# Moving the pool of small tiles ahead of the weight pools in a two-block network on one core

## The chip, the cores and the metric

The kernel runs on one core of a Trainium2 chip. The metric is device time in microseconds (us) of one execution of the whole kernel. Engines are written as in the profile: PE is TensorE (matmuls), PEld its loads of the stationary operand, DVE is VectorE, ACT is ScalarE, POOL is GpSimd, and SPq, ACTq and POOLq are the queues that issue DMAs.

## What is computed

The input is 512 tokens of width 1024, in float32. Two blocks follow each other. The first block is a dilated attention layer (three groups of eight heads, joined by their log-denominators, with a gate) and a differential attention layer (two softmaxes of which one is subtracted from the other), each between two RMS norms and with a residual. The second block is a feed-forward layer, a mixer of three gated branches (sparse attention with an index, a state-space layer, attention to 256 memory tokens), and a second feed-forward layer, with norms and residuals. Cut to what matters here, nearly all the arithmetic is projections of this form:

```python
def swiglu_ffn(h, w_in, w_out):
    gate, up = jnp.split(h @ w_in, 2, axis=-1)
    return (jax.nn.silu(gate) * up) @ w_out
...
x = x + 0.5 * swiglu_ffn(rms_norm(x, ffn1_norm[l]), ffn1_w_in[l], ffn1_w_out[l])
h = rms_norm(x, mix_norm[l])
q_a, k_a, v_a, q_i, k_i, w_i, u_s, q_m, gates = jnp.split(h @ w_in[l], offsets, axis=-1)
```

## The kernel before

**Projections.** Every product of an activation and a weight is made from three matmuls (`mm3`, lines 151 to 155): both operands are split into a high part h and a low part l in the type float32r, and h·h, h·l and l·h are added up in PSUM. Line 153 multiplies the high parts, line 154 and line 155 one high and one low part. A matmul has a stationary operand, which is loaded first (an LDWEIGHTS of 128 columns, shown as PEld), and a moving operand, which streams through. In the rows of the profile the moving operand is named first: `pp<-uh,wh` streams the activation uh past the weight wh, and `pp<-wh,uh` streams the weight past the activation.

There are two forms. `feat` (line 384) gives a feature-major result: the weight is stationary, 128 of its columns at a time, and 512 tokens of the activation move. `tok` (line 335) gives a token-major result: 128 tokens of the activation are stationary and up to 512 columns of the weight move. With `perm=True` (values of the dilated groups 1 and 2) the stationary tokens are taken four apart.

**Weights.** All weights come through one pipeline, in the order of a plan that is written out as the steps are set up. `_load` (line 291) issues, on the SP queue, the DMA of a piece of [128, 1024] into one of two buffers `raw`; `_split` (line 305) turns it into a pair `wh`, `wl` out of rings of four, with a cast on ACT (line 175) and a subtraction on DVE (line 176). A piece is split up to two pieces ahead of its use, and the load of a further piece is issued right after a split.

**Activations.** They lie transposed in rings `u` and `y` of [128, 4, 512] tiles (`uh`, `ul`, `yh`, `yl`). The 256 memory tokens have tiles of their own, `mT0h`, `mT0l`, `mT1h` and `mT1l`, of [128, 4, 256], out of the pool `aux` (line 1355); they are the stationary operand of one projection, `w_mem_kv`, in the form `tok`.

**Memory.** Pools are laid out end to end in each partition, in the order in which they are opened, and a pool that is opened takes its place behind those that are open. Lines 72 to 76 open the pools that stay open to the end:

```python
self.cpool = pool("consts", 1)
self.rings = {"u": pool("u", 2), "y": pool("y", 2)}
self.wraw = pool("wraw", RAW)
self.wsplit = pool("wsplit", RING)
self.small = pool("small", 2)
```

All other pools are opened later, behind `small`. `small` holds tiles of one to four numbers per partition (sums of squares, reciprocal roots), in 22 slots of 32 bytes, 704 bytes in all. Consts take 3,072 bytes, the four activation tags 16,384 each, `raw` 8,192, `wh` and `wl` 16,384 each. The places per partition that follow, in bytes:

| tile | first byte before | beyond a multiple of 128 |
|---|---|---|
| uh, ul, yh, yl | 19,584 / 35,968 / 52,352 / 68,736 | 0 |
| raw | 85,120 | 0 |
| wh, wl | 93,312 / 109,696 | 0 |
| small | 126,080 to 126,784 | 0 |
| mT0h, mT0l, mT1h, mT1l | 176,160 / 180,256 / 184,352 / 188,448 | 32 |

A piece of a matmul's operand is a whole number of times 512 bytes into its tile in nearly all cases: 128 stationary columns are 512 bytes. The exceptions are the projection of 452 columns (line 1462, `[(w, 512, 452)]`), whose second row of weights starts 1,808 bytes into the tile, and the stationary operand of the permuted form, whose columns are 16 bytes apart.

**Order of the work.** The host program emits the instructions in one order, with the estimated work of TensorE as its clock; side chains (attention, softmax, norms) are put between the matmuls of the projections by delays on that clock. Nothing in that order depends on where a tile lies.

## Time and profile before

| | |
|---|---|
| median of 3 runs | 2165.97 us (2165.5 to 2167.97) |
| profiled execution, first to last instruction | 2168.1 us |
| granted TensorE clock, mean | 0.994 |
| PE busy | 2108.8 us (97%), 10,217 matmul records |
| PEld busy | 1712.7 us (79%) |
| DVE busy | 1232.5 us (57%) |
| ACT busy | 938.7 us (43%) |
| POOL busy | 232.9 us (11%) |
| DMA | 204.11 MB, 94 GB/s on average |

The profiled execution's own time is known by its span alone, 2168.1 us, which is 2.1 us over the median of the runs. A matmul's duration in the profile (some 390 ns for 512 columns) is longer than the distance from one start to the next, since matmuls overlap; what the kernel pays for one matmul is the distance between starts, which the rows in order of time show.

### The profile page before, as it was taken

Reading aid. Unit: us, or ns where it says so; the run is one execution under the profiler, and the core shown is the slowest. Engines: PE = TensorE matmul, PEld = TensorE weight load, DVE = VectorE, ACT = ScalarE, POOL = GpSimd, SP = SyncE. Lnnn points to the kernel's source line nnn. Section 1 sums busy time; section 2 is a strip of 40 time slices with the busy share of each in tenths; the row PEclk is TensorE's granted clock in tenths of the full one; section 3 lists DMA queues with packets and bytes.
Section 4 is the critical chain, followed back from the end, with each engine's and each line's share of the span. In section 5 each row is a group of like instructions: output and inputs, shape, how many; then the busy total and the mean of one; then the engine's idle time right before and its main releaser. Section 6 shows DMA issues by size and latency. Waiting matters only on the chain.

```text
span 2168.1 us, 27642 instructions
## 1 busy us (share of the span) xinstructions
PE 2108.8 (97%) x10217; PEld 1712.7 (79%) x10217; DVE 1232.5 (57%) x2673; ACT 938.7 (43%) x1885; POOL 232.9 (11%) x322
## 2 busy tenths in 40 slices
PE   7999999999999999999999999988899999999998
PEld 6888988889888776788888888755567888888887
DVE  5645457454667677876443337889964345333334
ACT  4746455464545655555222224443344333223223
POOL 0000000000000000110960000125422110000000
PEclk9999999999999999999999999999999999999999
DMA  5322222212243212233343334222243323333332
GB/s 169 95 69 68 69 69 63 84 59 70 80 127 127 88 59 68 98 121 107 124 148 94 98 96 150 78 61 72 65 147 106 90 86 98 98 97 98 97 98 78
DMA packets 152055, 204.11 MB, mean 94 GB/s; under 512 B 9848, under 2 KB 111240, under 8 KB 151920
## 3 DMA queue, kind: packets, MB, share of 16 engines
q1 hardware_dynamic: 138368, 170.70, 25.8%
q10 hardware_dynamic: 8352, 15.14, 2.4%
q0 software_dynamic: 5200, 16.50, 2.2%
q8 instruction: 80, 1.31, 0.3%
q14 instruction: 55, 0.45, 0.1%
HBM read 191.80 MB, written 10.51 MB: 93 GB/s over the span
## 4 chain that ended last, share of the span: by engine, by line
PE 50%; DVE 8%; ACT 2%; issue 1%; DMA 1%; POOL 1%; ACTq 0%; DVEq 0%; POOLq 0%; SPq 0%
PE pp L153 15%; PE pp L154 15%; PE pp L155 15%; PE pa L159 3%; PE pa L164 2%; DVE wl L176 1%; DMA raw<-in_w_in 1%; DVE s5wr L1147 1%; DVE s5wi L1148 1%; DVE score L1262 1%; DVE m L1261 0%; DVE s5t L1150 0%; ACT p L438 0%; POOL s5wr L1142 0%; ACT wh L175 0%
## 5 line engine op out<-in xcount | busy, mean ns | idle before, releaser
L176 DVE TENSOR_TENSOR wl<-raw,wh 128x1024 fp32r<-128x1024 f32 (+1 forms) x320 | 407.1, 1273 | 495.5 <-ACT wh L175 494.2
L175 ACT CAST wh<-raw 128x1024 fp32r<-128x1024 f32 (+1 forms) x320 | 333.4, 1042 | 642.4 <-PE pp L154 291.3
L153 PE MATMUL pp<-uh,wh 128*128 128x512 f32 (+1 forms) x1232 | 485.1, 394 | 0.3 <-DVE sg L445 0.2
L154 PE MATMUL pp<-ul,wh 128*128 128x512 f32 (+1 forms) x1232 | 477.8, 388 | 1.0 <-DVE ul L282 1.0
L155 PE MATMUL pp<-uh,wl 128*128 128x512 f32 (+1 forms) x1232 | 477.8, 388 | 0.0
L153 PEld LDWEIGHTS pp<-uh,wh 128*128 128x128 f32 x1232 | 232.3, 189 | 52.0 <-issue 7.2
L155 PEld LDWEIGHTS pp<-uh,wl 128*128 128x128 f32 x1232 | 232.5, 189 | 45.9 <-issue 0.6
L154 PEld LDWEIGHTS pp<-ul,wh 128*128 128x128 f32 x1232 | 232.7, 189 | 43.7 <-DVE ul L282 1.2
L153 PE MATMUL pp<-wh,uh 128*128 128x512 f32 (+2 forms) x592 | 238.1, 404 | 0.0
L154 PE MATMUL pp<-wl,uh 128*128 128x512 f32 (+2 forms) x592 | 229.5, 388 | 0.2 <-DVE wl L176 0.2
L155 PE MATMUL pp<-wh,ul 128*128 128x512 f32 (+2 forms) x592 | 228.8, 387 | 0.0
L153 PE MATMUL pp<-yh,wh 128*128 128x512 f32 (+1 forms) x464 | 176.3, 380 | 0.8 <-DVE M L1497 0.8
L155 PE MATMUL pp<-yh,wl 128*128 128x512 f32 (+1 forms) x464 | 174.7, 377 | 0.0
L154 PE MATMUL pp<-yl,wh 128*128 128x512 f32 (+1 forms) x464 | 174.5, 376 | 0.0
L425 ACT COPY rq<-pp 32x512 f32<-32x512 f32 x256 | 147.8, 577 | 58.0 <-PE pp L155 52.8
L153 PEld LDWEIGHTS pp<-wh,uh 128*128 128x128 f32 x592 | 128.0, 216 | 20.3 <-issue 4.6
L154 PEld LDWEIGHTS pp<-wl,uh 128*128 128x128 f32 x592 | 128.5, 217 | 16.7 <-DVE wl L176 1.2
L155 PEld LDWEIGHTS pp<-wh,ul 128*128 128x128 f32 x592 | 127.6, 216 | 16.6 <-issue 0.3
L153 PE MATMUL pp<-wh,yh 128*128 128x512 f32 x304 | 119.1, 392 | 0.0
L154 PE MATMUL pp<-wl,yh 128*128 128x512 f32 x304 | 118.8, 391 | 0.0
L155 PE MATMUL pp<-wh,yl 128*128 128x512 f32 x304 | 118.7, 390 | 0.0
L438 ACT ACTIVATE sm<-sm,nm 128x128 f32<-128x128 f32 (+1 forms) x192 | 79.8, 417 | 54.4 <-DVE nm L437 54.1
(404 smaller groups left out, 2783.9 us busy)
## 6 DMA issues: line engine op xcount, KB each, us to landing
raw<-in_ffn_w_in SPq DMA_DIRECT2D x176, 256.0 KB, 3.1
raw<-in_dil_w_in SPq DMA_DIRECT2D x80, 512.0 KB, 3.6
raw<-in_ffn_w_out SPq DMA_DIRECT2D x44, 512.0 KB, 3.7
raw<-in_diff_w_in SPq DMA_DIRECT2D x32, 512.0 KB, 3.7
raw<-in_w_in SPq DMA_DIRECT2D x32, 512.0 KB, 3.7
raw<-in_dil_w_out SPq DMA_DIRECT2D x8, 512.0 KB, 3.7
raw<-in_diff_w_out SPq DMA_DIRECT2D x8, 512.0 KB, 3.7
s5tab<-s5cs POOLq DMA_DIRECT2D x8, 512.0 KB, 3.4
```

The lines of the kernel that those rows point to most:

```text
L153: mm(ps, a[0], b[0], start=first, stop=False)
L154: mm(ps, a[0], b[1], start=False, stop=False)
L155: mm(ps, a[1], b[0], start=False, stop=last)
L159: self.nc.tensor.matmul(ps, a, b, start=start, stop=stop)
L164: self.nc.tensor.transpose(ps, x, self.ident[:n, :n])
L175: self.nc.scalar.copy(h, src)
L176: return self.nc.vector.tensor_tensor(l, src, h.bitcast(F32), op=OP.subtract)
L425: nc.scalar.copy(sw[b:b + 32, :], ps[c][b ^ 32:(b ^ 32) + 32, :])
L438: nc.scalar.activation(sm, sm, AF.Exp, bias=nm, scale=-1.0, accum_out=den)
L1147: V.tensor_tensor_scan(wr, mag, wr, 0.0, op0=OP.mult, op1=OP.add)
L1148: V.tensor_tensor_scan(wi, mag, wi, 0.0, op0=OP.mult, op1=OP.add)
L1262: V.match_replace(sc[:, :n], m8, sc[:, :n], -BIG)
```

## The change

Two lines change places in what is computed: the pool `small` is opened before `wraw` and `wsplit`. The diff also takes comments and docstrings out (their lines stay as empty lines, so that line numbers hold).

```diff
         self.cpool = pool("consts", 1)
         self.rings = {"u": pool("u", 2), "y": pool("y", 2)}
+        self.small = pool("small", 2)
         self.wraw = pool("wraw", RAW)
         self.wsplit = pool("wsplit", RING)
-        self.small = pool("small", 2)
         self.pp = pool("pp", 4, space=PSUM)
```

So `raw`, `wh` and `wl` lie 704 bytes further on (85,824, 94,016 and 110,400), the tiles of `small` 40,960 bytes further back (at 85,120), and everything else, the rings of activations in front and all pools behind, where it was. 704 is five times 128 and 64 more.

## Rows read from the trace of the kernel before

**Rows 1.** The page: span, and busy time of each engine.
```profile
span 2168.1 us, 27642 instructions
...
PE 2108.8 (97%) x10217; PEld 1712.7 (79%) x10217; DVE 1232.5 (57%) x2673; ACT 938.7 (43%) x1885; POOL 232.9 (11%) x322
```

**Rows 2.** Busy time by stretch: length, PE, PEld, DVE, ACT, POOL, clock, DMA, GB/s.
```profile
960.00:1320.00 360.00, 359.68 (x1684) 300.19 (x1684) 161.97 (x242) 116.42 (x161) 100.46 (x171) 1.00 0.36 115
1345.00:1680.00 335.00, 305.83 (x1412) 216.97 (x1410) 270.44 (x634) 135.74 (x318) 101.56 (x99) 0.98 0.31 90
```

**Rows 3.** PE in order of time, first feed-forward: start, duration, line; 86 matmuls, first and last.
```profile
1130.69 0.39 PE L154 MATMUL pp<-ul,wh 128*128 128x512 f32 x1
...
1149.96 0.39 PE L155 MATMUL pp<-uh,wl 128*128 128x512 f32 x1
```

**Rows 4.** The same, second feed-forward, matmuls of 256 columns: 110, first and last.
```profile
1808.32 0.28 PE L155 MATMUL pp<-yh,wl 128*128 128x256 f32 x1
...
1821.40 0.28 PE L153 MATMUL pp<-yh,wh 128*128 128x256 f32 x1
```

**Rows 5.** The same, weight moving, activation stationary: 13 matmuls, first and last.
```profile
1182.14 0.39 PE L153 MATMUL pp<-wh,yh 128*128 128x512 f32 x1
...
1184.87 0.39 PE L153 MATMUL pp<-wh,yh 128*128 128x512 f32 x1
```

**Rows 6.** The same, weight moving, memory tile stationary: 13 matmuls, first and last.
```profile
1325.73 0.39 PE L153 MATMUL pp<-wh,mT0h 128*128 128x512 f32 x1
...
1328.53 0.39 PE L153 MATMUL pp<-wh,mT0h 128*128 128x512 f32 x1
```

**Rows 7.** The same, permuted form, stationary columns 16 bytes apart: 15 matmuls, first and last.
```profile
214.32 0.40 PE L155 MATMUL pp<-wh,ul 128*128 128x512 f32 x1
...
217.61 0.40 PE L154 MATMUL pp<-wl,uh 128*128 128x512 f32 x1
```

**Rows 8.** The same, 452 columns of weight moving: 18 matmuls, first and last.
```profile
1342.32 0.37 PE L153 MATMUL pp<-wh,uh 128*128 128x452 f32 x1
...
1345.79 0.37 PE L155 MATMUL pp<-wh,ul 128*128 128x452 f32 x1
```

**Rows 9.** The page, costliest groups: busy and mean ns, then idle time before.
```profile
L153 PE MATMUL pp<-uh,wh 128*128 128x512 f32 (+1 forms) x1232 | 485.1, 394 | 0.3 <-DVE sg L445 0.2
L153 PE MATMUL pp<-wh,uh 128*128 128x512 f32 (+2 forms) x592 | 238.1, 404 | 0.0
L153 PE MATMUL pp<-yh,wh 128*128 128x512 f32 (+1 forms) x464 | 176.3, 380 | 0.8 <-DVE M L1497 0.8
L153 PE MATMUL pp<-wh,yh 128*128 128x512 f32 x304 | 119.1, 392 | 0.0
```

**Rows 10.** Groups of the stretch 1345 to 1680, line 153, weight stationary.
```profile
L153 PE MATMUL pp<-uh,wh 128*128 128x512 f32 x147 | 61.7, 420 | 0.0
L153 PE MATMUL pp<-yh,wh 128*128 128x512 f32 x48 | 21.1, 443 | 0.8 <-DVE M L1497 0.8
```

**Rows 11.** Lines 175 and 176: durations ns min/median/max, first and last start, forms.
```profile
L175 ACT CAST wh<-raw x320: 602/1050/1077, 9.0 to 2139.0; 128x1024 fp32r<-128x1024 f32 x156, 128x904 fp32r<-128x904 f32 x2, 128x512 fp32r<-128x512 f32 x2
L175 ACT CAST yh<-sg x24: 387/617/621, 970.3 to 1292.0; 128x512 fp32r<-128x512 f32 x20, 128x256 fp32r<-128x256 f32 x4
L176 DVE TENSOR_TENSOR wl<-raw,wh x320: 679/1226/3009, 10.1 to 2140.1; 128x1024 fp32r<-128x1024 f32 x156, 128x904 fp32r<-128x904 f32 x2, 128x512 fp32r<-128x512 f32 x2
L176 DVE TENSOR_TENSOR yl<-sg,yh x24: 405/684/1774, 971.1 to 1293.6; 128x512 fp32r<-128x512 f32 x20, 128x256 fp32r<-128x256 f32 x4
```

**Rows 12.** The page, DMA issues: KB each, median us to landing.
```profile
raw<-in_diff_w_in SPq DMA_DIRECT2D x32, 512.0 KB, 3.7
s5cs<-s5tab ACTq DMA_DIRECT2D x8, 512.0 KB, 3.4
```

**Rows 13.** Waits, the SP queue's and PE's: us in total, times, longest.
```profile
SPq L300 <- DVE wl L176: 1546.0, 269, 25.3
...
PE pp L154 <- DVE wl L176: 0.2, 1, 0.2
```

## The prediction

> **What bounds the kernel now.** I read the page's busy times first. TensorE is busy 2108.8 of 2168.1 us and no other engine over 57% [rows 1], so a change counts by what it does to TensorE's spacing, or by a wait that it puts in front of TensorE. [...]

> Then the rows in order of time, for the price of one matmul from start to start. In the first feed-forward, 85 distances take 1149.96 - 1130.69 = 19.27 us, or 226.7 ns [rows 3]. With 256 columns, 109 distances take 13.08 us, or 120.0 ns [rows 4]. The 256 columns of difference cost 106.7 ns, which is one column per tick of 2.4 GHz; so 512 columns are 213.3 ns, and 13.3 ns stay as a pause that each matmul pays whatever its length. The pause is the same with the weight moving: twelve distances take 2.73 us [rows 5].

> Two stretches have another pause, and they are what this prediction turns on. Where the memory tiles are stationary, twelve distances take 2.80 us, 233.3 ns each [rows 6], with the same moving weights. The only thing I find that sets these matmuls apart is the place of the stationary operand, 32 bytes beyond a multiple of 128, where all activations and weights lie on one. In the permuted form, with the stationary columns 16 bytes apart, fourteen distances take 3.29 us, 235.0 ns each [rows 7]. So how the stationary operand lies in memory reaches the spacing: by 6.7 ns in one case, 8.3 ns in the other.

> **The change part by part.** No instruction is added, removed or moved, on an engine or a queue: the order is that of an emission which does not look at places. What changes is three addresses: raw, wh and wl start 64 bytes beyond a multiple of 128 instead of on one.

> Stationary weights. These are all matmuls of the form feat: per line of mm3 1,232 with uh and 464 with yh moving [rows 9], and three lines, so 3 x 1,696 = 5,088. No row of before has a float32r weight at 64 bytes beyond. The bounds are 0 (64 counts as on the grid) and 6.7 ns each (64 counts as the 32 of the memory tiles does). Nothing excludes a gain, but no row has a pause under 13.3 ns; a gain is taken up as a rival. I take the upper end, since the only contiguous stationary operand off 128 in the trace pays it, and all that are on 128 don't. In 1345 to 1680 us there are 3 x (147 + 48) = 585 of them [rows 10], in stretches with slack; I take 0 for these, with 585 x 6.7 ns = 3.9 us kept for the range. The other 4,503 stand back to back or nearly so: 4,503 x 6.67 ns = **30.0 us**. Nothing hides this, as TensorE is the bound there [rows 2].

> [...]

> Moving weights. The form tok has 592 with uh and 304 with yh per line [rows 9], 2,688 in all. The nearest row is the projection of 452 columns, in which half the moving weights start 1,808 bytes into a tile, 16 beyond a multiple of 128: 17 distances take 3.47 us, 204.1 ns; 452 columns are 188.3 ns, so the pause is 15.8 ns, 2.5 more than with all on 128 [rows 8]. If the half that is off bore it all, 5 ns each, 2,688 of them would cost 13.4 us; the lower bound is 0. I take 0: a length of 452 is itself odd, and a moving operand is one long stream in which the start matters little. The 13.4 us go to the range.

> Splits. The cast on ACT and the subtraction on DVE read and write tiles that all move together. A cast of 512 columns out of sg, which lies off 128 wherever it is placed, takes 617 ns, and the shortest out of raw, on 128, 602; the subtractions take 684 and 679 [rows 11]. So 15 ns and 5 ns per half piece are the upper bounds, 2 x 15 x 320 = 9.6 us of ACT and 3.2 us of DVE in all, and 0 the lower. I take 0: ACT and DVE work two pieces ahead, and TensorE waited 0.2 us once for a wl [rows 13]. Without that cover the 9.6 us would be paid.

> Loads. A 512 KB load into raw lands in 3.7 us, one of the same size into s5cs, which lies off 128, in 3.4 [rows 12]. So I take 0, with 0.3 us per load either way as the bound. The SP queue spends 1546 us waiting until DVE has freed a raw [rows 13], so loads have time to spare; that is the cover, and the split's lead of two pieces behind it.

> Small tiles. They move by 40,960 bytes, which is 320 x 128: nothing changes in how they lie, cost 0.

> Sum: 2168.1 + 30.0 = 2198.1 us on the profiled execution's span; that execution stands 2.1 us over the median of the runs shown, so 2166 + 30 = **2196 us** as a median.

> **The rivals.** *No change: 64 bytes are enough of a grid.* If what counts is a multiple of 64 (or less), the memory tiles pay because 32 is no multiple of 64, and weights at 64 beyond pay nothing. For it: both 32 and 64 are unknown steps, and the trace has one value only. It is also the outcome if another trait of the memory tiles (how far they lie from the weights, what else runs in that stage) makes their 6.7 ns, or if the shift does not reach the matmuls as the code says. Time 2166, 2162 to 2170. [...] *Both operands pay.* What counts is how the stationary and the moving operand lie to each other, so that tok pays as well: 4,503 + 2,688 = 7,191 times 6.7 ns, 48 us, 2214; or tok by the bound of [rows 8], 13.4 us, 2209. Against it: the 452 columns, whose weights lie 16 bytes off their activations and pay at most 5 ns. *Faster.* The pause of 13.3 ns is itself a clash of two streams that start alike, and an offset of 64 bytes takes half of it away: 6.7 ns less in 4,503 matmuls, 30 us, 2136. It decides as soon as a distance under 226.7 ns appears in the first feed-forward. Against it: neither offset in the trace, 32 for the stationary nor 16 for the moving operand, brought the pause down.

> **How the numbers follow.** Stationary weights pay: 0.48. Both pay: 0.06. No change: 0.38. Faster: 0.08. The first two are slower, 0.54. A measurement of this kernel can tell about 0.2% (4 us) from no change, so the shares stand as faster 0.08, same 0.38, slower 0.54. The range runs from the lower edge of "no change", 2162, to the forecast with the 3.9 us of the slack stretches and half of the moving operand's 13.4 us on top, some 2206; outside lie the 0.08 of faster and the 0.06 of both. The forecast's own range is 2185 to 2206, its lower end being two thirds of the price, where disturbed matmuls next to attention work pay nothing.

> **What would show it.** In the profile after, the same count of 27,642 instructions, and in the first feed-forward a distance of 233.3 ns where the weight is stationary, beside 226.7 where it moves. The memory tiles' stretch should stay at 233.3 if the stationary operand's place alone counts, and may move if it is the offset between both operands. ACT's casts stay at 1050 ns, DVE's subtractions at 1226, loads at 3.7 us. I am wrong if the weight-stationary distance stays at 226.7 (no change), falls (faster), or if the time goes up with these distances unchanged, which would mean a wait for loads or splits that I have put at nothing.

## The result and the profile after

The changed kernel takes 2187.28 us (2186.61 to 2189.62, 4 runs) against 2165.73 us before (4 runs): a ratio of 1.0097 with a 95% interval of 1.0083 to 1.0111, so 21.5 us slower, where 30 were forecast. The instructions of every engine stand in the same order as before.

The page after, span and busy time of each engine:

```profile
span 2185.4 us, 27642 instructions
...
PE 2126.9 (97%) x10217; PEld 1708.9 (78%) x10217; DVE 1227.7 (56%) x2673; ACT 938.4 (43%) x1885; POOL 233.6 (11%) x322
```

And the same two stretches as in [rows 2], with the same columns (length, PE, PEld, DVE, ACT, POOL, clock, DMA, GB/s):

```profile
960.00:1320.00 360.00, 358.54 (x1660) 295.85 (x1659) 155.48 (x231) 116.00 (x162) 100.47 (x169) 1.00 0.35 112
1345.00:1680.00 335.00, 303.84 (x1407) 215.88 (x1406) 270.78 (x639) 136.42 (x316) 98.77 (x97) 0.98 0.31 92
```

TensorE is busy 18.1 us longer than in [rows 1], no other engine by more than 0.7 us. The clock is as granted before, 1.00 and 0.98. But the same 360 us hold 1,660 matmuls instead of 1,684 [rows 2], with TensorE as good as always busy: on average a matmul takes longer.

Which ones, the rows in order of time show, as in [rows 3] (start, duration, line, operands with the moving one first). First, the first feed-forward with the weight stationary and uh moving, 84 matmuls:

```profile
1130.80 0.39 PE L153 MATMUL pp<-uh,wh 128*128 128x512 f32 x1
...
1149.80 0.39 PE L155 MATMUL pp<-uh,wl 128*128 128x512 f32 x1
```

Then the weight moving, the counterpart of [rows 5], 70 matmuls:

```profile
1189.85 0.39 PE L153 MATMUL pp<-wh,yh 128*128 128x512 f32 x1
...
1205.95 0.40 PE L153 MATMUL pp<-wh,yh 128*128 128x512 f32 x1
```

And in the second feed-forward the weight stationary again, with yh moving, 85 matmuls:

```profile
1982.22 0.40 PE L155 MATMUL pp<-yh,wl 128*128 128x512 f32 x1
...
2001.82 0.40 PE L155 MATMUL pp<-yh,wl 128*128 128x512 f32 x1
```

The distance from start to start is 19.00 / 83 = 228.9 ns in the first, 16.10 / 69 = 233.3 ns in the second and 19.60 / 84 = 233.3 ns in the third. Before, the first had 226.7 [rows 3]. The second begins with the row at 1182.14 of [rows 5], and its 70th matmul is the first row below: 15.65 / 69 = 226.8. The other two rows are the third before, the same 85 matmuls: 19.04 / 84 = 226.7.

```profile
1197.79 0.39 PE L153 MATMUL pp<-wh,yh 128*128 128x512 f32 x1
...
1969.20 0.39 PE L155 MATMUL pp<-yh,wl 128*128 128x512 f32 x1
...
1988.24 0.39 PE L155 MATMUL pp<-yh,wl 128*128 128x512 f32 x1
```

So the form in which the weight moves pays the full 6.6 to 6.7 ns, though the prediction gave it nothing, and the form in which it is stationary pays 2.2 ns in one place and 6.7 in another.

The memory tiles, stationary as in [rows 6], keep their distance: 13 matmuls after, 2.80 / 12 = 233.3 ns.

```profile
1336.15 0.39 PE L153 MATMUL pp<-wh,mT0h 128*128 128x512 f32 x1
...
1338.95 0.39 PE L153 MATMUL pp<-wh,mT0h 128*128 128x512 f32 x1
```

What does not move are the splits and the loads. The cast has a median of 1048 ns and the subtraction of 1225, against 1050 and 1226 [rows 11]. Lines 175 and 176 after:

```profile
L175 ACT CAST wh<-raw x320: 601/1048/1077, 8.8 to 2155.7; 128x1024 fp32r<-128x1024 f32 x156, 128x904 fp32r<-128x904 f32 x2, 128x512 fp32r<-128x512 f32 x2
...
L176 DVE TENSOR_TENSOR wl<-raw,wh x320: 676/1225/2353, 9.8 to 2156.8; 128x1024 fp32r<-128x1024 f32 x156, 128x904 fp32r<-128x904 f32 x2, 128x512 fp32r<-128x512 f32 x2
```

The loads land in 3.6 us, against 3.7 [rows 12]. From the page's DMA issues after:

```profile
raw<-in_diff_w_in SPq DMA_DIRECT2D x32, 512.0 KB, 3.6
```

**The account.** I took all distances under 260 ns between neighbouring matmuls of mm3 with 512 moving columns, from both traces, and multiplied the difference of the means by the number before. Weight moving: 227.4 to 233.3 ns, 2,016 times (33 of them past the memory tiles), 12.0 us. Permuted form: 235.4 to 237.9, 330 times, 0.8 us. Weight stationary, uh moving: 227.8 to 229.3, 3,162 times, 4.9 us. Weight stationary, yh moving: 227.0 to 230.6, 1,136 times, 4.0 us. Matmuls of fewer columns come to 0.2 us in all. That makes 21.9 us by means. The order of the matmuls is the same in both traces, so each distance can also be paired with its own counterpart. Paired so, these distances grew by 22.6 us, and the 3,018 that hold other work or a wait shrank by 5.1: together 17.5 us from TensorE's first start to its last, beside 17.3 us between the two spans. The rest up to 21.5 us lies in the choice of executions. A run's time is some 1.8 us more than its span wherever both are known (2187.24 and 2185.4 us for the one profiled after). By that the one profiled before, known by its span alone, took about 2169.9 us, an estimate, which is 4.2 us over its median and not the 2.1 that comes of setting a span beside a time; the one profiled after stands at its own median.

### The profile page after: what moved, and what is told of

It is laid out like the page before. It is cut to its first block, busy times and chain, and to the rows that moved or that the text cites. A ratio compares the mean times of both kernels' runs of the same rounds, so it can differ in the third digit from the quotient of the medians.

```text
span 2185.4 us, 27642 instructions
## 1 busy us (share of the span) xinstructions
PE 2126.9 (97%) x10217; PEld 1708.9 (78%) x10217; DVE 1227.7 (56%) x2673; ACT 938.4 (43%) x1885; POOL 233.6 (11%) x322
## 4 chain that ended last, share of the span: by engine, by line
PE 51%; DVE 8%; ACT 1%; DMA 1%; issue 1%; POOL 1%; ACTq 0%; DVEq 0%; SPq 0%; POOLq 0%
PE pp L153 15%; PE pp L154 15%; PE pp L155 15%; PE pa L159 3%; PE pa L164 2%; DVE wl L176 1%; DVE s5wr L1147 1%; DVE s5wi L1148 1%; DMA raw<-in_w_in 0%; DVE m L1261 0%; DVE score L1262 0%; DVE s5t L1150 0%; ACT p L438 0%; POOL s5wr L1142 0%; ACT wh L175 0%
## 5 line engine op out<-in xcount | busy, mean ns | idle before, releaser
L176 DVE TENSOR_TENSOR wl<-raw,wh 128x1024 fp32r<-128x1024 f32 (+1 forms) x320 | 400.9, 1253 | 508.4 <-ACT wh L175 507.4
L155 PEld LDWEIGHTS pp<-uh,wl 128*128 128x128 f32 x1232 | 232.8, 189 | 46.8 <-issue 0.6
L155 PE MATMUL pp<-wh,ul 128*128 128x512 f32 (+2 forms) x592 | 230.6, 390 | 0.0
L153 PEld LDWEIGHTS pp<-yh,wh 128*128 128x128 f32 x464 | 87.2, 188 | 21.4 <-issue 3.9
```

What stands on the lines that cost most here:

```text
L153: mm(ps, a[0], b[0], start=first, stop=False)
L155: mm(ps, a[1], b[0], start=False, stop=last)
L176: return self.nc.vector.tensor_tensor(l, src, h.bitcast(F32), op=OP.subtract)
```

## The experiments

Three theories stood at the start. **A:** what counts is how the two operands of a matmul lie to each other. **B:** each operand counts for itself, by its distance from a multiple of 128; this was the prediction's, with the moving operand added to it. **C:** the matmuls alone don't show it; something that runs beside them makes it. A fourth, **D**, blames the small tiles or the distance of 704 bytes itself.

**Matmuls alone** (scan). Streams of 48 matmuls in the pattern of mm3, one after another, out of tiles of 16,384 bytes per partition:

```diff
+    def stream(so, mo, n, two=True):
+        ps = pp.tile([P, 512], F32, name="ps", tag="ps")
+        so, mo = so // 4, mo // 4
+        for i in range(N):
+            k = i // 3 % 6
+            a, b = (("sh", "mh"), ("sh", "ml"), ("sl", "mh"))[i % 3]
+            nc.tensor.matmul(ps[:, :n], t[a][:, k * P + so:k * P + so + P], t[b][:, k * 512 + mo:k * 512 + mo + n],
+                             start=i == 0, stop=i == N - 1)
+        return ps
```

> This kernel leaves all of the network out but its matmuls: 45 streams of 48 float32r matmuls each, nothing else running, with the stationary tiles s bytes and the moving tiles m bytes beyond a multiple of 128. Theory A (what counts is how the two operands lie to each other, modulo 128): 226.7 ns from start to start wherever s and m are alike (0/0, 32/32, 64/64, 96/96, and offsets of 128 or 256), and more elsewhere, 229 to 233.3 ns at s=64, m=0 and at s=0, m=64, 233.3 ns at s=32, m=0. Theory B (each operand for itself): 233.3 ns in the whole row s=32, the cost of m=64 the same at every s, and no return to 226.7 ns at 64/64. Theory C (the place plays no part, the slowdown after the change comes from what runs beside the matmuls): 226.7 ns everywhere. Streams of 256 columns: 120.0 ns at 0/0, about 118 ns at s=64 and 115.5 ns at m=64 if the matmuls alone make what the changed kernel shows.

Measured in one execution, mean distance in ns with 512 columns, the first matmuls of each stream left out; the stationary offset s goes down and the moving offset m across, both in bytes:

| s \ m | 0 | 32 | 64 | 96 |
|---|---|---|---|---|
| 0 | 226.7 | 233.3 | 228.9 | 233.2 |
| 32 | 233.3 | 226.7 | 233.3 | 228.9 |
| 64 | 233.3 | 233.3 | 226.7 | 233.3 |
| 96 | 234.3 | 233.3 | 233.3 | 226.7 |

The rows behind three of its fields, in order of time (39, 39 and 38 matmuls): s=0 with m=64, s=64 with m=64, and s=64 with m=0.

```profile
69.72 0.39 PE L32 MATMUL ps<-ml,sh 128*128 128x512 f32 x1
...
78.42 0.39 PE L32 MATMUL ps<-mh,sh 128*128 128x512 f32 x1
...
158.61 0.39 PE L32 MATMUL ps<-ml,sh 128*128 128x512 f32 x1
...
167.22 0.39 PE L32 MATMUL ps<-mh,sh 128*128 128x512 f32 x1
...
136.24 0.39 PE L32 MATMUL ps<-ml,sh 128*128 128x512 f32 x1
...
144.87 0.39 PE L32 MATMUL ps<-mh,sl 128*128 128x512 f32 x1
```

8.70 / 38 = 228.9, 8.61 / 38 = 226.6 and 8.63 / 37 = 233.2 ns. The diagonal is at 226.7 whatever the common offset: A holds in this, B falls, and C falls with the three values of the kernels before and after appearing when nothing else runs. The sign counts too: m - s = 64 costs 2.2 ns, m - s = -64 costs 6.7. But A's period of 128, which the expectation took for granted, is refuted: m = 128 gives 233.3, s = 128 gives 233.3, and only 256 is back at 226.7 (226.9 at m = 256). An offset of 192 of the stationary operand gives 229.0, as m - s = 64 does, and of the moving one 233.3, as -64 does.

So 704 = 2 x 256 + 192 puts the weights at -64 from the activations, modulo 256. Where the weight moves, m - s = -64, which is 233.3; where it is stationary, m - s = 64, which is 228.9. These are the two values of the first feed-forward. With 256 columns the order is reversed: 120.1 ns at 0/0, 117.8 at s=64 and at m=64 (where 115.5 was expected), 113.3 at m=16.

**Activations and weights moved together** (all_alike).

```diff
+        self.small = pool("small", 2)
         self.rings = {"u": pool("u", 2), "y": pool("y", 2)}
         self.wraw = pool("wraw", RAW)
         self.wsplit = pool("wsplit", RING)
-        self.small = pool("small", 2)
```

> The pool of small tiles is opened ahead of the activations as well, so that activations and weights all lie 64 bytes beyond a multiple of 128. Theory A (operands to each other): the time of before, 2166 us, and 226.7 ns in both forms. Theory B (each operand for itself): both operands are off in every matmul, so no less than the change, 2187 us, and by adding up both prices about 2200 us.

Measured: 2169.87 us against 2169.03 before on that chip, a ratio of 1.0004 (0.9994 to 1.0014). The first feed-forward is back at the distance of before, 19.27 us for 85 distances, 226.7 ns:

```profile
1130.67 0.39 PE L153 MATMUL pp<-uh,wh 128*128 128x512 f32 x1
...
1149.94 0.39 PE L154 MATMUL pp<-ul,wh 128*128 128x512 f32 x1
```

Both operands lie 64 bytes beyond a multiple of 128 here, and nothing is paid: A, not B. The small tiles moved further than in the change, too.

**64 bytes instead of 704** (shift64). One tag of the small tiles, 64 bytes, stays ahead of the weights:

```diff
         self.rings = {"u": pool("u", 2), "y": pool("y", 2)}
+        self.front = pool("front", 2)
         self.wraw = pool("wraw", RAW)
...
-        m = self.small.tile([P, 2], F32, name="rms", tag="rms", bufs=2)
+        m = self.front.tile([P, 2], F32, name="rms", tag="rms", bufs=2)
```

> Only one tag of small tiles (64 bytes) is put ahead of the weights, which move by 64 bytes instead of 704. Theories A and B: the time of the changed kernel, 2187 us, with 233.3 ns where weights move. Theory D (704 bytes as a distance, or the 40,960 bytes by which the small tiles move): the time of before, 2166 us.

Measured: 2195.76 us, a ratio of 1.0123 (1.0107 to 1.0138). D falls, since the small tiles hardly moved. But it is dearer than the change, which no theory had said, and the period of 256 says why: 64 is +64 where 704 was -64, and the two forms change places. The added line makes lines 154 to 156 those of mm3 here. The weight stationary, 83 matmuls, then moving, 70: 19.13 / 82 = 233.3 and 15.80 / 69 = 229.0 ns.

```profile
1130.81 0.40 PE L156 MATMUL pp<-uh,wl 128*128 128x512 f32 x1
...
1149.94 0.40 PE L154 MATMUL pp<-uh,wh 128*128 128x512 f32 x1
...
1195.45 0.39 PE L154 MATMUL pp<-wh,yh 128*128 128x512 f32 x1
...
1211.25 0.39 PE L154 MATMUL pp<-wh,yh 128*128 128x512 f32 x1
```

Over the whole trace, the means as in the account are 233.3 ns where the weight is stationary and 229.3 where it moves, and there are nearly twice as many of the former.

**640 bytes** (shift640). The other way round: all small tags but that one are ahead of the weights.

```diff
         self.rings = {"u": pool("u", 2), "y": pool("y", 2)}
+        self.small = pool("small", 2)
         self.wraw = pool("wraw", RAW)
         self.wsplit = pool("wsplit", RING)
-        self.small = pool("small", 2)
+        self.back = pool("back", 2)
...
-        m = self.small.tile([P, 2], F32, name="rms", tag="rms", bufs=2)
+        m = self.back.tile([P, 2], F32, name="rms", tag="rms", bufs=2)
```

> All small tiles but that one tag are put ahead of the weights, which move by 640 bytes, five times 128. Theories A and B with a grid of 128: the time of before, 2166 us, within 0.2%. With a coarser grid (256 or 512 bytes): something else, between 2166 and 2200 us. Theory D (the distance or the small tiles): the time of the change, 2187 us.

Measured: 2201.17 us, a ratio of 1.0144 (1.0128 to 1.016), the slowest of all. 640 = 2 x 256 + 128, and 128 costs the same in both directions: means of 232.8 ns with uh moving and 232.9 where the weight moves. For the latter, 70 matmuls, 16.10 / 69 = 233.3 ns:

```profile
1197.29 0.40 PE L154 MATMUL pp<-wh,yh 128*128 128x512 f32 x1
...
1213.39 0.39 PE L154 MATMUL pp<-wh,yh 128*128 128x512 f32 x1
```

A grid of 128 is refuted in the kernel itself.

The theory that was left is **E**: the place of the moving operand less that of the stationary one, modulo 256, sets the distance. Its rivals were **F**, that any shift of the weights costs, as all three tried so far did, and **G**, that the raw tile's part in loads and casts bears some of it.

**256 bytes** (shift256). Two tags of the small tiles, 256 bytes in all, ahead of the weights:

```diff
+        self.front = pool("front", 2)
         self.wraw = pool("wraw", RAW)
...
-        m = self.small.tile([P, 2], F32, name="rms", tag="rms", bufs=2)
+        m = self.front.tile([P, 2], F32, name="rms", tag="rms", bufs=2)
...
-        return self.small.tile([P, 2], F32, name="ss", tag="ss", bufs=6)
+        return self.front.tile([P, 2], F32, name="ss", tag="ss", bufs=6)
```

> Two tags of small tiles, 256 bytes in all, are put ahead of the weights, which move by 256 bytes. Theory E (the place of the moving operand less that of the stationary one, modulo 256, sets the pause): the time of before within 0.2%, and 226.7 ns in both forms. Theory F (any shift of the weights against the activations costs, as 64, 640 and 704 bytes all did): about 1 to 1.5% slower, 2187 to 2200 us.

Measured: 2168.48 us, a ratio of 0.9999 (0.999 to 1.0009), and 19.27 us for 85 distances in the first feed-forward, as before:

```profile
1130.65 0.39 PE L155 MATMUL pp<-ul,wh 128*128 128x512 f32 x1
...
1149.92 0.39 PE L156 MATMUL pp<-uh,wl 128*128 128x512 f32 x1
```

F falls, and E holds as to which shift is free. How much the others cost it does not settle alone, as the last section shows.

**Only wh and wl moved** (split_only), and **only raw moved** (raw_only).

```diff
         self.wraw = pool("wraw", RAW)
+        self.small = pool("small", 2)
         self.wsplit = pool("wsplit", RING)
-        self.small = pool("small", 2)
```

> The pool of small tiles is opened between the raw weights and the split ones: only wh and wl move by 704 bytes, raw stays where it was, so loads land as before. Theory E: the whole of the change's cost, a ratio of 1.010 (2187 us), with 233.3 ns where weights move and 229 to 230.5 ns where they are stationary. Theory G (loads or casts bear part of the cost): clearly under 1.010.

```diff
-        self.wraw = pool("wraw", RAW)
         self.wsplit = pool("wsplit", RING)
         self.small = pool("small", 2)
+        self.wraw = pool("wraw", RAW)
```

> The raw weights are put behind the small tiles: raw lies 64 bytes beyond a multiple of 128, wh and wl stay on a multiple of 256 from the activations. Theory E: the time of before within 0.2%, 226.7 ns in both forms. Theory G (loads or casts bear part of the cost): slower by 0.2% or more, with loads over 3.7 us or casts over 1050 ns.

Measured: split_only 2188.69 us, a ratio of 1.0092 (1.0077 to 1.0107), raw_only 2169.86 us, 1.0008 (0.9998 to 1.0017). The whole cost comes with wh and wl, and none that can be told from zero with raw: G falls. In raw_only the cast, which now reads from 64 beyond a multiple of 128 and writes to a tile on one, takes 1049 ns, and the load 3.7 us; line 175 and the DMA issues of raw_only:

```profile
L175 ACT CAST wh<-raw x320: 602/1049/1076, 8.7 to 2137.6; 128x1024 fp32r<-128x1024 f32 x156, 128x904 fp32r<-128x904 f32 x2, 128x512 fp32r<-128x512 f32 x2
```

```profile
raw<-in_diff_w_in SPq DMA_DIRECT2D x32, 512.0 KB, 3.7
```

**A finer search, with high and low tiles apart** (scan2). The same streams, now of 36, with an offset for each of the four tiles, and a width w of the stationary operand:

```diff
+            nc.tensor.matmul(ps[:w, :n], t[a][:, k * P + off[a]:k * P + off[a] + w],
+                             t[b][:, k * 512 + off[b]:k * 512 + off[b] + n], start=i == 0, stop=i == N - 1)
```

> This kernel leaves all of the network out but its matmuls: 60 streams of 36, nothing else running, with the high and the low tiles of each operand placed on their own, in steps of 8 bytes. Theory E with a period of 256: 226.7 ns at offsets of 256, 512 and 1024, 229 ns at 64 and 320-like remainders, 233.3 ns at 192 (448, 704, 960), and no offset under 226.7 ns for 512 columns. If the clash is between a matmul's stream and the load of the next stationary operand, high and low tiles need only agree each with its own kind: 226.7 ns with both low tiles moved by 32, 64 or 128 bytes together. If it is between a matmul's stream and its own stationary operand, these cost some 2 to 7 ns in every third matmul or in two of three. The pause of 13.3 ns: if the load's reads make it, it falls with fewer stationary columns; if it is a fixed cost of a matmul, it stays at 13.3 ns from 256 to 512 columns and at every width.

Measured in one execution, with both moving tiles at m and both stationary ones at 0: 226.6 to 226.7 ns at m = 240, 256, 512 and 1024; 233.3 at 192, 448, 704 and 960; 229.0 at 64; about 231 to 237 at all other multiples of 8 up to 248. Nothing lies clearly under 226.7 for 512 columns, so no offset that was tried beats the kernel before in its main stream. With both low tiles moved together by 32, 64 or 128 bytes against both high ones the means are 232.1, 230.9 and 231.2 ns: it is not enough that each kind agrees with itself. Nor does a matmul's own pair settle it alone. With only the low moving tile moved by 64 bytes, two matmuls in three have m - s = 0 and the third 64, which by the values above would make 227.5 ns on average; the mean is about 232. Fewer loaded columns do not shorten the pause: 32, 64 and 96 stationary columns give 231.7, 230.0 and 230.0 ns, more than the 226.6 of 128. And the pause, at the prediction's 106.7 ns per 256 columns, is 13.3 ns with 256 and 384 moving columns (119.9 and 173.3 ns) but 20.0 with 448 (206.7) and 16.8 with 496 (223.5), so that the length of the stream counts as well as its start.

## Why the prediction was right, and where it was wrong

*What bounds the kernel:* right. The growth is in TensorE's distances, 17.5 us by the account, and the forecast's sign, its range and its own range (2185 to 2206) hold 2187.3.

*Where the difference comes from:* here a term failed, or rather two that lean against each other. "Stationary weights" was put at 30.0 us, 6.7 ns in 4,503 matmuls. The trace shows 8.9 us: 1.5 ns on average with uh moving and 3.5 with yh. "Moving weights" was put at 0, with 13.4 us kept for the range, on the ground that the start of a long stream matters little. It was 12.8 us with the permuted form. The sum of the two came near what was measured because their errors have opposite signs, and that is luck.

The step behind both is the reading of the memory tiles [rows 6]. The prediction took "32 beyond a multiple of 128" as a trait of the stationary operand, since all others lay on 128. It was a trait of the pair. In those rows the weights lie 128 beyond a multiple of 256 and the memory tiles 32 beyond one, so m - s is 96, for which the scan has 233.2 ns. After the change the weights are at 64 and m - s is 32, at 233.3, which is why that stretch kept its distance: the mean of its distances is 233.1 ns before and 233.3 after. The rival "Both operands pay" had the mechanism, at a chance of 0.06, with a price of 48 us that the kernel does not reach: one of its two forms pays a third of it in most places, and the waits give some back. The 452 columns [rows 8], which I held against that rival, tell nothing of it. Among their distances under 260 ns in the trace before, those that begin with weights 1,808 bytes into the tile, 16 beyond a multiple of 256, have a mean of 203.5 ns (48 distances), those with weights at its start 204.5 (44): the half that is off is not the dearer one. The 231.6 ns of the scan for m = 16, 4.9 over the best, are with 512 columns and every moving operand off, and scan2 has a pause of 20.0 ns at 448 columns with no offset at all.

A smaller slip is in the count. Of the 5,088 weight-stationary matmuls 384 have 256 columns; [rows 9] has them under "+1 forms", and no row gave a price for these. In the scan an offset of 64 makes that length cheaper, 117.8 ns against 120.1.

*Slack:* right for the stretch that was named, in which TensorE is idle for 29.2 of 335 us [rows 2]. In it the 393 close distances with the weight stationary did not grow (0.0 us in sum), and the whole stretch grew by 1.6 us. The 5.1 us by which the distances with other work or a wait shrank over the whole kernel were in no term.

*Splits, loads, small tiles at nothing:* right, shown by raw_only (1.0008) and all_alike (1.0004).

*No change and faster:* the former would have been true for a shift by a multiple of 256. The latter never showed for 512 columns, at any of the offsets in steps of 8 bytes. It is real for 256 columns in the scan (120.1 to 113.3 ns), which are 3 x 160 of the kernel's matmuls, too few to count.

*The pause:* the 13.3 ns rest on the 106.7 ns that 256 columns more take, [rows 3] against [rows 4], which is 2.4 columns per ns. That a column takes one tick of the clock is the prediction's reading of this; the runs show the granted share of the clock, not its frequency. Nor is the pause the same whatever the length: scan2 has 13.3 ns at 256 and 384 columns, but 20.0 at 448 and 16.8 at 496.

## What to carry to other kernels

In a stream of float32r matmuls that bounds a kernel, the places of stationary and moving tiles are worth a look: a multiple of 256 bytes between them was free in every run here (226.6 to 226.9 ns in the scans, a ratio of 0.9999 in shift256), so put pools of odd size ahead of both (1.0004 in all_alike) or behind both. A distance from start to start that is a few ns over that of its neighbours in the same trace (233.3 against 226.7 here) is worth explaining by comparing the operands' addresses as a pair; a trait of one operand is easily mistaken for the cause when the other never varies. Two shifts of the same sort may differ in sign (704 bytes left -64 and cost 1.0%, 64 bytes left +64 and cost 1.2%), so test a multiple of the suspected period and a half of it before naming the period.

## What the runs showed of the hardware that was not expected

```profile
41.70 0.39 PE L153 MATMUL pp<-uh,wh 128*128 128x512 f32 x1
...
87.02 0.39 PE L153 MATMUL pp<-uh,wh 128*128 128x512 f32 x1
...
41.52 0.40 PE L153 MATMUL pp<-uh,wh 128*128 128x512 f32 x1
...
87.72 0.40 PE L153 MATMUL pp<-uh,wh 128*128 128x512 f32 x1
```

- Two more values of the scans do not follow from the difference alone: m = 48 gives 230.0 ns in scan and 233.3 in scan2, and m = 240 gives 226.6 ns, but s = 16 with m = 0, the same modulo 256, gives 233.3.
- The load of the stationary operand shows none of it: its mean duration for `pp<-uh,wh` is 189 ns in both profiles.
- What clashes inside TensorE or its memory at these offsets is not shown by any run; the offsets, lengths and widths above are what is known.
